# A feed-forward's output projection with held two-tile look-ahead, and modulation steps spread over its input products

## The chip, the cores and the metric

The kernel runs on one core of one Trainium2 chip. The metric is the device time of one execution in microseconds (us), as the median of several.

## What is computed

One layer of a diffusion backbone over 256 context and 512 latent tokens, 768 rows in all, with a model width of 1024. The part around the change is the first feed-forward, run on all 768 rows, and the modulation vectors of the later parts:

```python
mod = (sc @ w_mod[l] + b_mod[l]).reshape(-1, N_MOD, D_MODEL)      # 9 vectors of 1024, sc = silu(c)
modc = (scc @ w_mod[l] + b_mod[l]).reshape(1, N_MOD, D_MODEL)     # the same for the context rows
x = ada_out(x, swiglu(ada_in(x, mod, 0, norm_pre[l, 0]), ffn_w_in[l, 0], ffn_w_out[l, 0]),
            mod, 0, norm_post[l, 0], 0.5)
def swiglu(y, w_in, w_out):
    a, b = jnp.split(y @ w_in, 2, axis=-1)     # w_in 1024 x 5632
    return (jax.nn.silu(a) * b) @ w_out        # w_out 2816 x 1024
```

Behind it come the mLSTM and pooling mixer and a second feed-forward on the 512 latent rows. All of it is float32.

## The kernel before, in words

**Float32 products from parts.** Every operand of a large product is split into a high part (`split_hi`, a cast on ScalarE, line 81 in the profile's L81) and a low part (`split_lo`, a subtraction on VectorE, L78), and each product is three matmuls (`mm3`, L97 to L99; `mm3p`, L102, is the same with its order on TensorE held). So each weight tile costs one load of 512 KB, one cast and one subtraction before TensorE can use it.

**Input products (`Ffn.in_fast`, L359).** The hidden width of 2816 is 22 tiles `f` of 128. Tiles 3 to 21 go through `in_fast`: seven products of half size (a fast 2 x 2 matrix product) in place of eight, 84 matmuls of 384 columns. Sums of weight quarters come first (`first_sums`, `last_sums`), then their splits; a tile's split weights take 7 of the 8 buffers of tag `win`. The results are put together by VectorE additions (L379, L384, L388, L389, L392) and a multiplication (L393) and stored to DRAM as `g_f` (L490).

**Modulation steps (`mod_steps`, L666).** Seven blocks of 1024 modulation values (blocks 2 to 8) are computed on VectorE as a Python generator of 70 steps, ten to a block. Each of the first eight steps of a block loads 512 KB of `w_mod` into one of six `m4` buffers (L675) and issues one VectorE multiply-add (L677) for each stream: two streams (latent and context) for blocks 2 to 4, one for blocks 5 to 8. Step nine issues nothing; step ten issues eight matmuls with a vector of ones (L687), one scaling, and stores of the row. When block 4 is done, `begin_chain` prepares the parameters of the stage's end (eight transposes and eight small matmuls on TensorE, two loads of 256 KB and two row broadcasts). `filler(n)` takes n steps; it is called after each `in_fast` tile (two steps after tiles 4 to 11, three after tiles 12 to 21) and once after each output tile.

**Output projection (`out_pass`, L740).** Two passes, each over half of the rows (384) and over all 22 tiles, accumulate in six PSUM banks: 18 matmuls of 512 columns for each tile. `prepare(f)` loads and splits the weights `wos[f]` (load L748, unless they are kept from the first pass) and the hidden values `g_f` (load L751, into a buffer of tag `q3`). In the kernel before it stands right in front of the tile's products. The second pass begins with the four tiles whose weights are still in place. At the end of a pass, `done1` and `ada_tile` form the normalised rows of the next stage: squares (L148), scalings (L175, L179, L187), and for each row tile two "back" steps, each with four transposes on TensorE (L105), four activations on ScalarE (L199), a cast (L203) and a subtraction (L204). `Backs.tick` lets these steps run later, between the following tiles: one falls at the end of the first pass, five between the first tiles of the second.

**What sets the order.** The kernel is written for a tracing compiler that orders each engine's instructions itself: among those that its own estimate holds ready, the one traced first goes first. `keep_in_program_order` (in the code `pin`, `mm`, `tp`) holds an instruction behind the others so marked on its engine; `issue_after(ins)` keeps what a block issues on `ins`'s engine behind `ins`. Once built, each engine runs its list strictly in order, and so does the DMA queue of SP that issues nearly all loads and stores.

Of the kernel before, what the change touches and what calls it, by code (L numbers as in the profile page):

```python
# [8 lines left out]
F32 = mybir.dt.float32  # L9
# [34 lines left out]
def tile_layer(ctx: ExitStack, tc: tile.TileContext, x, c, ctxt, c_ctx, w_mod, b_mod, norm_pre, norm_post,  # L44
# [35 lines left out]
    def split_hi(src, hi):  # L80
        return S.copy(hi, src)  # L81

    def split_lo(src, hi, lo):
        return sub_to(V, lo, src, hi.bitcast(F32))
# [1 line left out]
    def part(pool=wpool, tag="win", n=D):  # L86
        return pool.tile([P, WIDE if tag == "win" else D], F32R, tag=tag, name=tag + "s")[:, 0:n]

    def split_w(src, pool=wpool, tag="win", to=None):

        hi, lo = to or (part(pool, tag), part(pool, tag))
        split_hi(src, hi)
        split_lo(src, hi, lo)
        return hi, lo

    def mm3(out_ap, wh, wl, xh, xl, first, last, **kw):
# [69 lines left out]
    x1_d = [dpool.tile([P, D], F32, name=f"x1_{t}") for t in range(4)]  # L166
    x2_d = [dpool.tile([P, D], F32, name=f"x2_{t}") for t in range(4)]

    def ada_tile(t, zs, z, halves, xr, gc, store, nxt, junk, half):


        r = rstd2(halves)
        parts = ([slice(0, D)] if zs is None else [slice(h * 512, (h + 1) * 512) for h in range(2)])
        for h, cs in enumerate(parts):
            mul = V.tensor_mul(z[:, cs], z[:, cs] if zs is None else zs[h], gc[:, cs])  # L175
            if nxt is None and t == NTT - 1:
                tc.keep_in_program_order(mul)
        for cs in parts:
            V.scalar_tensor_tensor(out=z[:, cs], in0=z[:, cs], scalar=r, in1=xr[:, cs], op0=ALU.mult, op1=ALU.add)  # L179
            if nxt is None:  # L180
                load(store[:, cs], z[:, cs])
        if nxt is None:
            return None
        if store is not None:
            load(store, z)
        r2 = rstd1(z, junk)
        V.tensor_scalar_mul(xr, z, r2)  # L187
        scale, shift = nxt
        ts = slice(t * P, (t + 1) * P)

        def back(q):
            yf = half()
            p = pt()
            for j in range(4):
                k = 4 * q + j
                tp(out=p[:, j * P:(j + 1) * P], in_=xr[:, k * P:(k + 1) * P], identity=ident)
            for j in range(4):
                k = 4 * q + j
                S.activation(out=yf[:, j * P:(j + 1) * P], in_=p[:, j * P:(j + 1) * P], func=AF.Identity,  # L199
                             scale=scale[:, k:k + 1], bias=shift[:, k:k + 1])  # L200
            ks = slice(4 * q, 4 * q + 4)
            ysrc = kc(yf)
            S.copy(yh[:, ks, ts], ysrc)  # L203
            V.tensor_sub(yl[:, ks, ts], ysrc, yh[:, ks, ts].bitcast(F32))  # L204

        return back

# [31 lines left out]
    class Ffn:  # L239
        def __init__(self, wi, wo_ap, tiles, c_lo, c_hi):  # L240
            self.wi, self.wo_ap, self.tiles, self.c_lo = wi, wo_ap, tiles, c_lo
            self.ncol = c_hi - c_lo
            self.g, self.w, self.wo, self.fast = {}, {}, {}, False

        def scope(self, pool, done, filler, junk):
            self.pool, self.done, self.filler, self.junk = pool, done, filler, junk
# [112 lines left out]
        def in_fast(self, f, between=lambda: None):  # L359

            n = self.n
            (xh, xl), (sh, sl), (uh, ul), x22p = self.w.pop(f, None) or self.last_sums(self.first_sums(f))
            lo, hi = slice(0, 512), slice(512, 1024)

            def product(q, wh, wl, y, first=True):
                wh, wl, (mh, ml) = kc(wh), kc(wl), self.moving[y]
                for k in range(4):
                    mm3(q[:, 0:n], wh[:, k], wl[:, k], mh[:, k], ml[:, k], first and k == 0, k == 3,
                        skip_group_check=not first)

            sg, cb, pu, pv = (self.two(x) for x in ("s", "cb", "pu", "pv"))
            p1, u2, p5, u3 = pu[:, 0:n], pu[:, n:2 * n], pv[:, 0:n], pv[:, n:2 * n]
            qa, qc, qb = pa(), pa(), pa()
            product(qa, xh[:, lo], xl[:, lo], "y11")
            S.copy(p1, qa[:, 0:n])
            product(qc, sh[:, lo], sl[:, lo], "t1")
            S.copy(p5, qc[:, 0:n])
            product(qb, sh[:, hi], sl[:, hi], "t2")
            V.tensor_add(u2, p1, qb[:, 0:n])  # L379
            between()  # L380
            product(qa, xh[:, hi], xl[:, hi], "y21", False)
            S.activation(out=sg[:, 0:n], in_=qa[:, 0:n], func=AF.Silu)
            product(qc, uh[:, hi], ul[:, hi], "y22", False)
            V.tensor_add(sg[:, n:2 * n], u2, qc[:, 0:n])  # L384
            S.activation(out=sg[:, n:2 * n], in_=sg[:, n:2 * n], func=AF.Silu)
            qd = pa()
            product(qd, uh[:, lo], ul[:, lo], "t3")
            V.tensor_add(u3, u2, qd[:, 0:n])  # L388
            V.tensor_add(cb[:, n:2 * n], u3, p5)  # L389
            qe = pa()  # L390
            product(qe, x22p[:, lo], x22p[:, hi], "t4")
            V.tensor_add(cb[:, 0:n], u3, qe[:, 0:n])  # L392
            V.tensor_mul(cb, cb, sg)  # L393
            self.finish(f, cb)
# [58 lines left out]
    with ExitStack() as sx:  # L453
        pool = sx.enter_context(tc.tile_pool(name="ffn1", bufs=6))

        def m4(dt=F32):
            return pool.tile([P, D], dt, tag="m4", name="m4")

        def q3(dt=F32):
            return pool.tile([P, NT], dt, tag="q3", name="q3", bufs=10)  # L460

        def sw(dt=F32):
            return pool.tile([P, D], dt, tag="sw", name="sw", bufs=2)
# [5 lines left out]
        def done1(t, qs, z, halves, xr):  # L469
            st = 1 if t < 2 else 0  # L470
            load(xr, ctxt[t * P:(t + 1) * P, :] if t < 2 else x[(t - 2) * P:(t - 1) * P, :])
            return ada_tile(t, qs, z, halves, xr, chain["g"][st], None if t < 2 else x1_d[t - 2], chain["y"][st], junk,
                            lambda: q3()[:, 0:512])

        blocks1 = ((0, 384), (384, 384))
        f1 = Ffn(ffn_w_in[0], ffn_w_out[0], range(NTT), 0, NT)
# [50 lines left out]
                    ws.append(r)  # L527
            return ws

        pin = tc.keep_in_program_order  # L530
        bgv = bg.rearrange("p (g k o) -> p g k o", g=3, o=1)

        class Split:
# [172 lines left out]
        steps = mod_steps()  # L706

        def filler(n):
            with tc.issue_after(sums_end.ins):
                for _ in range(n):  # L710
                    if next(steps, None) == 4:
                        begin_chain()

        def begin_chain():
            mix_params()
            query_key()
            chain["g"] = [bc_row(m4(), (2, st)) for st in range(2)]
            cols = columns("ycol1", [(4, 0), (3, 0), (4, 1), (3, 1)])
            chain["y"] = [(cols[0], cols[1]), (cols[2], cols[3])]
# [10 lines left out]
        with tc.issue_after(last_y.ins):  # L730
            f1.w[3] = f1.last_sums(f1.first_sums(3, raws3))
        sums_end = rest()
        for f in range(3, NF):
            f1.in_fast(f)
            filler(3 if f >= 12 else 2 if f > 3 else 0)


        wos = {}
# [1 line left out]
        def out_pass(half, order, tail, homes, z, xr, before, backs):  # L740
            c0 = 384 * half
            qs = [(pa(), pa()), (pa(), pa()), (pz(), pz())]
            gs = {}

            def prepare(f):
                if f not in wos:
                    r = raw()
                    load(r, f1.wo_ap[f * P:(f + 1) * P, :])  # L748
                    wos[f] = split_w(r, to=homes[f]() if f in homes else None)
                r = q3()[:, 0:384]  # L750
                load(r, g_d[f][:, c0:c0 + 384])  # L751
                g = q3(F32R)
                gs[f] = split_w(r, to=(g[:, 0:384], g[:, 384:NT]))

            def product(f, i, h, mm3):
                (gh, gl), (wh, wl) = gs[f], wos[f]
                ts, cs = slice(i * P, (i + 1) * P), slice(512 * h, 512 * h + 512)
                mm3(qs[i][h], gh[:, ts], gl[:, ts], wh[:, cs], wl[:, cs], f == order[0], f == order[-1])

            for f in order[:-tail]:  # L760
                prepare(f)
                for i in range(3):
                    for h in range(2):
                        product(f, i, h, mm3)
                before.tick()
                filler(1)
            for f in order[-tail:]:
                prepare(f)
            for i in range(3):
                t, halves = 3 * half + i, small(2)  # L770
                for h in range(2):
                    for f in order[-tail:]:
                        product(f, i, h, mm3p)
                    square_to(halves[:, h:h + 1], qs[i][h], junk[:, 512 * h:512 * h + 512])
                    backs.tick()
                backs.add(done1(t, qs[i], z[:, i], halves, xr(i)))

        def rows3(tag):
            return pool.tile([P, 3, D], F32, tag=tag, name=tag + "z", bufs=1)
# [1 line left out]
        backs, first_backs = Backs(4), Backs(4)  # L781
        xr1 = rows3("tl")
        order = list(range(NF))
        out_pass(0, order, 2, {}, rows3("th"), lambda i: xr1[:, i], Backs(0), first_backs)
        for f in order[:-4]:
            wos.pop(f)
        order = order[-4:] + order[-5::-1]
# [606 lines left out]
```

## Time and profile before

| | us |
|---|---|
| median of 3 runs | 1189.13 |
| lowest, highest | 1185.16, 1192.81 |
| the profiled execution, own time | 1192.41 |
| its span, first to last instruction | 1190.7 |
| mean granted TensorE clock over the span | 0.978 of full speed |

Times in the rows below are counted from the start of the span of the profiled execution. A wait is put down to the instruction that ended it (behind the arrow `<-`). The granted clock is a share of full speed; 1.00 is 2.4 GHz, 0.50 is 1.2 GHz. A few per cent of the matmul records may be missing, so counts of matmuls are a little low.

### The profile page before, as it was taken

To read this page: it belongs to the slowest core of one execution; us is meant where nothing else is said; L and a number is where in the kernel's file an instruction comes from. 1 tells how busy PE (TensorE), PEld (TensorE's weight loads), DVE (VectorE), ACT (ScalarE), POOL (GpSimd) and SP (SyncE) were. 2 spreads that over 40 slices of the span, in tenths; PEclk is the share of its full clock that TensorE was granted. 3 is DMA by queue.
4 is the path that set the end of the run, shared out by engine and by line. 5 is a ranking of instruction groups with operands and counts; after the bars stand their busy time and mean duration, and the time that the engine had idled before them with its cause. 6 is when DMAs were issued, how large, how long until landed. Compare 5 with 4: busy or idle time off the path is not lost.

```text
span 1190.7 us, 17232 instructions
## 1 busy us (share of the span) xinstructions
PE 1123.2 (94%) x6610; PEld 1012.6 (85%) x6610; DVE 895.5 (75%) x1315; ACT 530.3 (45%) x910; POOL 104.6 (9%) x139
## 2 busy tenths in 40 slices
PE   4999999997999999779999799999999999999996
PEld 3899999996999787557889688887989999999995
DVE  3799988989798756424553877785899998888865
ACT  4544333341434333434455466556664444444431
POOL 4000000000000000100020505421000000000001
PEclk9999999998999999889999899999999999999999
DMA  9934436354576887335642211224334433333321
GB/s 300 297 103 133 132 107 217 103 169 141 155 226 227 294 290 254 123 101 178 210 126 58 58 45 63 80 89 142 126 101 121 132 107 107 107 107 107 98 80 72
DMA packets 152672, 169.25 MB, mean 142 GB/s; under 512 B 7414, under 2 KB 125686, under 8 KB 152588
## 3 DMA queue, kind: packets, MB, share of 16 engines
q1 hardware_dynamic: 152540, 168.12, 44.5%
q8 instruction: 52, 0.85, 0.3%
q14 instruction: 32, 0.26, 0.1%
q10 hardware_dynamic: 48, 0.01, 0.0%
HBM read 153.12 MB, written 14.98 MB: 141 GB/s over the span
## 4 chain that ended last, share of the span: by engine, by line
PE 78%; DVE 8%; issue 4%; ACT 4%; POOL 3%; DMA 1%; DVEq 0%; ACTq 0%; POOLq 0%; SPq 0%
PE pa L98 16%; PE pa L97 16%; PE pa L99 16%; PE pa L102 8%; PE pz L102 5%; PE pz L97 4%; PE pz L98 4%; PE pz L99 4%; PE pt L102 2%; DVE m L677 2%; DVE wins L78 1%; PE pt L105 1%; ACT wins L81 1%; POOL sm L143 1%; ACT q L199 1%
## 5 line engine op out<-in xcount | busy, mean ns | idle before, releaser
L98 PE MATMUL pa<-yh,wins 128*128 128x256 f32 (+1 forms) x768 | 238.4, 311 | 2.7 <-DVE wins L78 2.7
L78 DVE TENSOR_TENSOR wins<-raw,wins 128x1024 fp32r<-128x1024 f32 (+1 forms) x145 | 158.0, 1090 | 107.9 <-ACT wins L81 75.7
L97 PE MATMUL pa<-yh,wins 128*128 128x256 f32 (+1 forms) x768 | 238.1, 310 | 0.7 <-ACT yh L81 0.4
L99 PE MATMUL pa<-yl,wins 128*128 128x256 f32 (+1 forms) x768 | 238.1, 310 | 0.0
L81 ACT CAST wins<-raw 128x1024 fp32r<-128x1024 f32 (+1 forms) x147 | 136.7, 936 | 130.8 <-PE pz L98 69.9
L98 PEld LDWEIGHTS pa<-yh,wins 128*128 128x128 f32 x768 | 146.5, 191 | 5.1 <-DVE wins L78 4.6
L97 PEld LDWEIGHTS pa<-yh,wins 128*128 128x128 f32 x768 | 146.2, 190 | 4.3 <-issue 2.1
L99 PEld LDWEIGHTS pa<-yl,wins 128*128 128x128 f32 x768 | 146.6, 191 | 0.5
L97 PE MATMUL pa<-th,wins 128*128 128x384 f32 (+1 forms) x388 | 121.8, 315 | 0.7 <-ACT wins L81 0.7
L99 PE MATMUL pa<-tl,wins 128*128 128x384 f32 (+1 forms) x388 | 122.4, 316 | 0.0
L98 PE MATMUL pa<-th,wins 128*128 128x384 f32 (+1 forms) x388 | 122.1, 315 | 0.0
L81 ACT CAST wins<-sw 128x1024 fp32r<-128x1024 f32 x78 | 81.7, 1048 | 54.1 <-DVE sw L78 34.1
L78 DVE TENSOR_TENSOR wins<-sw,wins 128x1024 fp32r<-128x1024 f32 x78 | 95.4, 1223 | 10.3 <-PE pa L98 7.0
L677 DVE SCALAR_TENSOR_TENSOR m<-m,sc,m 128x1024 f32<-128x1024 f32 x80 | 101.2, 1281 | 2.5 <-DMA m<-in_w_mod_dram 2.3
L102 PE MATMUL pa<-yh,wins 128*128 128x512 f32 (+2 forms) x352 | 96.8, 362 | 0.0
L97 PE MATMUL pa<-wins,q 128*128 128x512 f32 x152 | 60.0, 412 | 19.6 <-ACT q L81 19.6
L97 PEld LDWEIGHTS pa<-th,wins 128*128 128x128 f32 x388 | 73.1, 189 | 1.2 <-ACT wins L81 1.1
L99 PEld LDWEIGHTS pa<-tl,wins 128*128 128x128 f32 x388 | 73.3, 189 | 0.1
L98 PEld LDWEIGHTS pa<-th,wins 128*128 128x128 f32 x388 | 73.3, 189 | 0.0
L102 PEld LDWEIGHTS pa<-yh,wins 128*128 128x128 f32 x352 | 61.8, 190 | 9.1 <-issue 2.2
L98 PE MATMUL pa<-wins,q 128*128 128x512 f32 x152 | 63.8, 420 | 1.0 <-DVE q L78 1.0
L99 PE MATMUL pa<-wins,q 128*128 128x512 f32 x152 | 63.1, 415 | 0.0
(376 smaller groups left out, 2176.8 us busy)
## 6 DMA issues: line engine op xcount, KB each, us to landing
raw<-in_ffn_w_in_dram SPq DMA_DIRECT2D x87, 512.0 KB
raw<-in_ffn_w_out_dram SPq DMA_DIRECT2D x62, 512.0 KB
m<-in_w_mod_dram SPq DMA_DIRECT2D x57, 512.0 KB
g<-q SPq DMA_DIRECT2D x22, 384.0 KB
q<-g SPq DMA_DIRECT2D x44, 192.0 KB
raw<-in_w_in_dram SPq DMA_DIRECT2D x16, 512.0 KB
raw<-in_w_mod_dram SPq DMA_DIRECT2D x11, 512.0 KB
raw<-in_w_out_dram SPq DMA_DIRECT2D x16, 256.0 KB
```

What stands on the lines that cost most here:

```text
L78: return eng.tensor_tensor(out=out_ap, in0=a, in1=b, op=ALU.subtract)
L81: return S.copy(hi, src)
L97: T.matmul(out_ap, lhsT=wh, rhs=xh, start=first, stop=False, **kw)
L98: T.matmul(out_ap, lhsT=wl, rhs=xh, start=False, stop=False, **kw)
L99: T.matmul(out_ap, lhsT=wh, rhs=xl, start=False, stop=last, **kw)
L102: return tc.keep_in_program_order(T.matmul(*args, **kw))
L105: return tc.keep_in_program_order(T.transpose(**kw))
L143: G.tensor_tensor(out=r, in0=ms, in1=mhalf[:, 0:n], op=ALU.pow)
L199: S.activation(out=yf[:, j * P:(j + 1) * P], in_=p[:, j * P:(j + 1) * P], func=AF.Identity, scale=scale[:, k:k + 1], bias=shift[:, k:k + 1])
L677: V.scalar_tensor_tensor(out=accs[st], in0=w, scalar=sc[:, st * KD + k:st * KD + k + 1], in1=accs[st], op0=ALU.mult, op1=ALU.add)
```

## The change

`split_w` and `ada_tile` get a `keep` argument, by which the splits of `out_pass` and the activations, casts and subtractions of the back steps are held in program order on ScalarE and VectorE. In `out_pass`, the first two tiles are prepared ahead of the loop, and inside it tile `f + 2` is prepared before the products of tile `f`. In the first pass, tile 0's weights go to the two `sw` buffers, which held weight sums before, in place of `win` buffers.

The modulation steps of the input products no longer come in groups after a tile. `in_fast` calls `self.tick` after two of its VectorE additions (L379 and L389); three of every four calls take a single step, whose VectorE instructions are kept behind that addition. That makes 27 steps in tiles 4 to 21 instead of 46. The first pass of the output projection takes two steps after every third tile and one after the others (27 instead of 20), and the second pass the remaining 16 instead of 4. The old order of all steps behind `sums_end` is dropped.

```diff
-    def split_w(src, pool=wpool, tag="win", to=None):
+    def split_w(src, pool=wpool, tag="win", to=None, keep=lambda ins: ins):
         hi, lo = to or (part(pool, tag), part(pool, tag))
-        split_hi(src, hi)
-        split_lo(src, hi, lo)
+        keep(split_hi(src, hi))
+        keep(split_lo(src, hi, lo))
...
     def ada_tile(..., half, keep=lambda ins: ins):      # done1 passes pin
-                S.activation(out=yf[...], in_=p[...], func=AF.Identity, ...)
+                keep(S.activation(out=yf[...], in_=p[...], func=AF.Identity, ...))
-            S.copy(yh[:, ks, ts], ysrc)
-            V.tensor_sub(yl[:, ks, ts], ysrc, yh[:, ks, ts].bitcast(F32))
+            keep(S.copy(yh[:, ks, ts], ysrc))
+            keep(V.tensor_sub(yl[:, ks, ts], ysrc, yh[:, ks, ts].bitcast(F32)))
...
     in_fast:
-            V.tensor_add(u2, p1, qb[:, 0:n])
+            self.tick(V.tensor_add(u2, p1, qb[:, 0:n]))
...
-            V.tensor_add(cb[:, n:2 * n], u3, p5)
+            self.tick(V.tensor_add(cb[:, n:2 * n], u3, p5))
...
         def filler(n):
-            with tc.issue_after(sums_end.ins):
-                for _ in range(n):
-                    if next(steps, None) == 4:
-                        begin_chain()
+            for _ in range(n):
+                if next(steps, None) == 4:
+                    begin_chain()
...
-        for f in range(3, NF):
+        f1.in_fast(3)
+        count = iter(range(100))
+
+        def mod_tick(ins):
+            if next(count) % 4 < 3:
+                with tc.issue_after(ins.ins):
+                    filler(1)
+
+        f1.tick = mod_tick
+        for f in range(4, NF):
             f1.in_fast(f)
-            filler(3 if f >= 12 else 2 if f > 3 else 0)
...
-                    wos[f] = split_w(r, to=homes[f]() if f in homes else None)
+                    wos[f] = split_w(r, to=homes[f]() if f in homes else None, keep=pin)
...
-                gs[f] = split_w(r, to=(g[:, 0:384], g[:, 384:NT]))
+                gs[f] = split_w(r, to=(g[:, 0:384], g[:, 384:NT]), keep=pin)
...
-            for f in order[:-tail]:
+            for f in order[:2]:
                 prepare(f)
+            for f, later in zip(order[:-tail], order[2:]):
+                prepare(later)
                 for i in range(3):
                     for h in range(2):
                         product(f, i, h, mm3)
                 before.tick()
-                filler(1)
-            for f in order[-tail:]:
+                filler(2 if half == 0 and f % 3 == 0 else 1)
+            for f in order[len(order) - tail + 2:]:
                 prepare(f)
...
-        out_pass(0, order, 2, {}, rows3("th"), lambda i: xr1[:, i], Backs(0), first_backs)
+        out_pass(0, order, 2, {0: lambda: (sw(F32R), sw(F32R))}, rows3("th"), lambda i: xr1[:, i], Backs(0), first_backs)
```

## Rows read from the trace of the kernel before

**Rows 1.** Windows by stage: PE, PEld, DVE, ACT, POOL busy us (count), clock, DMA, GB/s.

```profile
278.00:304.00 26.00, 18.60 (x68) 16.24 (x68) 22.51 (x26) 6.65 (x10) 0.00 (x0) 0.74 0.30 99
392.30:486.70 94.40, 92.55 (x408) 74.35 (x404) 58.14 (x65) 33.11 (x51) 2.61 (x5) 1.00 0.79 271
486.70:544.00 57.30, 37.68 (x136) 28.00 (x137) 21.16 (x30) 23.98 (x52) 3.92 (x8) 0.82 0.33 110
```

**Rows 2.** Waits of PE, 250 to 396 us: total, times, longest, in us.

```profile
PE pt L687 <- issue: 4.0, 1, 4.0
PE pa L98 <- DVE wins L78: 2.7, 2, 2.3
PE pa L97 <- ACT q L81: 1.8, 1, 1.8
PE pa L97 <- ACT wins L81: 0.7, 1, 0.7
```

**Rows 3.** Timeline of DVE and PE: start, duration, instruction, count, idle before.

```profile
275.46 4.87 DVE L677 SCALAR_TENSOR_TENSOR m<-m,sc,m 128x1024 f32<-128x1024 f32 x4
...
281.52 0.69 PE L98 MATMUL pa<-yh,wins 128*128 128x384 f32 x1 [2.26 <-DVE wins L78]
```

**Rows 4.** Windows of line L677 alone: length, DVE busy (count), clock, DMA, GB/s.

```profile
265.00:294.50 29.50, 18.85 (x16) 0.88 0.41 136
107.10:392.30 285.20, 78.14 (x62) 0.98 0.52 167
392.30:486.70 94.40, 20.50 (x16) 1.00 0.79 271
```

**Rows 5.** ACT timeline, first copy (L375) of two neighbouring input tiles.

```profile
121.80 0.48 ACT L375 COPY q<-pa 128x384 f32<-128x384 f32 x1 [1.02 <-PE pa L99]
...
136.54 0.48 ACT L375 COPY q<-pa 128x384 f32<-128x384 f32 x1 [1.01 <-PE pa L99]
```

**Rows 6.** Window of two tile periods without modulation steps; columns as rows 1.

```profile
159.20:188.68 29.48, 29.48 (x171) 28.39 (x170) 21.04 (x30) 11.07 (x17) 0.00 (x0) 1.00 0.48 157
```

**Rows 7.** Windows at half and at full clock; columns as rows 1.

```profile
280.73:287.56 6.83, 6.04 (x19) 6.04 (x20) 4.75 (x6) 1.46 (x2) 0.00 (x0) 0.50 0.38 119
294.39:301.21 6.82, 6.36 (x16) 4.66 (x17) 6.75 (x8) 1.59 (x3) 0.00 (x0) 0.50 0.24 78
306.00:312.83 6.83, 6.83 (x41) 6.83 (x40) 5.32 (x8) 2.87 (x5) 0.00 (x0) 1.00 0.26 78
502.60:509.43 6.83, 5.94 (x14) 4.69 (x15) 1.16 (x2) 0.83 (x2) 0.00 (x0) 0.50 0.34 106
523.08:526.49 3.41, 3.41 (x10) 2.65 (x9) 0.00 (x0) 0.00 (x0) 0.00 (x0) 0.50 0.77 270
548.00:554.83 6.83, 6.83 (x31) 5.54 (x30) 2.41 (x4) 2.95 (x4) 0.00 (x0) 1.00 0.71 233
```

**Rows 8.** Waits of PE, 476 to 545 us: total, times, longest, in us.

```profile
PE pa L97 <- ACT q L81: 17.8, 6, 3.7
```

**Rows 9.** Timeline of SP and ACT around one stall of the second pass.

```profile
502.68 0.38 SPq L751 DMA_DIRECT2D q<-g  x1
...
510.43 1.04 ACT L81 CAST wins<-raw 128x1024 fp32r<-128x1024 f32 x1 [6.99 <-PE pz L98]
511.38 1.50 ACT L199 ACTIVATE q<-pt,ycol 128x128 f32<-128x128 f32 x4
512.91 0.62 ACT L203 CAST yh<-q 128x512 fp32r<-128x512 f32 x1
513.43 0.51 ACT L81 CAST q<-q 128x384 fp32r<-128x384 f32 x1
```

**Rows 10.** DMA view of the first pass, 392.3 to 486.7 us.

```profile
DMA packets 9391, 25.56 MB, mean 271 GB/s; under 512 B 1151, under 2 KB 4262, under 8 KB 9385
```

**Rows 11.** The busiest window of the first pass; columns as rows 1.

```profile
410.00:420.00 10.00, 10.00 (x45) 8.11 (x44) 7.84 (x9) 3.79 (x5) 0.00 (x0) 1.00 1.00 376
```

**Rows 12.** Waits of the SP queue, 107.1 to 392.3 us: total, times, longest.

```profile
SPq L675 <- DVE m L677: 51.9, 21, 7.2
```

More of the change, by code (lines that the diff above doesn't have):

```diff
@@ L167, in tile_layer, with ada_tile @@
     x2_d = [dpool.tile([P, D], F32, name=f"x2_{t}") for t in range(4)]
-    def ada_tile(t, zs, z, halves, xr, gc, store, nxt, junk, half):
+    def ada_tile(t, zs, z, halves, xr, gc, store, nxt, junk, half, keep=lambda ins: ins):
         r = rstd2(halves)
@@ L198, in back @@
                 k = 4 * q + j
-                S.activation(out=yf[:, j * P:(j + 1) * P], in_=p[:, j * P:(j + 1) * P], func=AF.Identity,
-                             scale=scale[:, k:k + 1], bias=shift[:, k:k + 1])
+                keep(S.activation(out=yf[:, j * P:(j + 1) * P], in_=p[:, j * P:(j + 1) * P], func=AF.Identity,
+                                  scale=scale[:, k:k + 1], bias=shift[:, k:k + 1]))
             ks = slice(4 * q, 4 * q + 4)
             ysrc = kc(yf)
-            S.copy(yh[:, ks, ts], ysrc)
-            V.tensor_sub(yl[:, ks, ts], ysrc, yh[:, ks, ts].bitcast(F32))
+            keep(S.copy(yh[:, ks, ts], ysrc))
+            keep(V.tensor_sub(yl[:, ks, ts], ysrc, yh[:, ks, ts].bitcast(F32)))
         return back
@@ L242, in __init__ @@
             self.ncol = c_hi - c_lo
-            self.g, self.w, self.wo, self.fast = {}, {}, {}, False
+            self.g, self.w, self.wo, self.fast, self.tick = {}, {}, {}, False, lambda ins: None
         def scope(self, pool, done, filler, junk):
@@ L457, in m4 @@
             return pool.tile([P, D], dt, tag="m4", name="m4")
+        pin = tc.keep_in_program_order
         def q3(dt=F32):
@@ L472, in done1 @@
             return ada_tile(t, qs, z, halves, xr, chain["g"][st], None if t < 2 else x1_d[t - 2], chain["y"][st], junk,
-                            lambda: q3()[:, 0:512])
+                            lambda: q3()[:, 0:512], pin)
         blocks1 = ((0, 384), (384, 384))
@@ L528, in mod_loads @@
             return ws
-        pin = tc.keep_in_program_order
         bgv = bg.rearrange("p (g k o) -> p g k o", g=3, o=1)
```

## The prediction

> **What bounds the kernel now.** I read the profile's page first: TensorE (PE) is busy in nearly every slice, but its row dips twice in the part that the change touches, and the granted clock dips with it. The windows by stage then price the dips [rows 1]: in 278 to 304 us PE is busy for 18.60 of 26.00 us at a mean clock of 0.74 while VectorE (DVE) is busy for 22.51; in 486.7 to 544 us, where the second output pass begins, PE is busy for 37.68 of 57.30. Between them, in the first output pass, PE is busy for 92.55 of 94.40. So PE bounds this part, and it loses time at three places; the waits of PE, the timelines and the waits by name tell why.
>
> *Input products.* PE waits four times [rows 2]: 4.0 for the matmuls that end a modulation block (L687), 2.7 in two waits for weight splits on DVE, 0.7 for a cast; the 1.8 belongs to the output projection. The timeline shows the cause of the longest split wait [rows 3]: four modulation multiply-adds in a row, 4.87 us, stand on DVE before the split, and PE is idle for 2.26. The steps come in clumps, 16 multiply-adds in 29.5 us [rows 4]. One tile takes 14.74 us of PE (the same copy at 121.80 and 136.54, [rows 5]). Without modulation DVE works 21.04 us in two such periods, 10.52 a tile [rows 6]. A multiply-add takes 78.14 / 62 = 1.26 us [rows 4]. Two two-stream steps a tile make 10.52 + 4 x 1.26 = 15.6 us, three make 18.1: both over 14.74.
>
> *Clock.* After the idle 2.26 us the granted clock is 0.50, which is 1.2 of 2.4 GHz, from 280.73 for 6.83 us, and again from 294.39 behind the 4.0 wait [rows 7].
>
> *Second pass.* PE waits six times, 17.8 us in total, for the same thing, a cast of `g` on ScalarE (ACT) [rows 8]. One stall is enough to see why [rows 9]: SP issued that load at 502.68, the tile began with the cast at 513.43, and what stood ahead of it on ACT was the back step's four activations (1.50) and its cast (0.62), which wait for PE's transposes. The data had 10 us to land; ACT's order was late.
>
> **The change part by part.** The sum is made in the profiled execution's own time, 1192.41 us (span 1190.7 and 1.71 around it), which is 3.28 above the median of 1189.13 and within the runs' spread.
>
> (a) *Single steps.* Three of four additions let a step in, so 1.5 a tile: DVE has 10.52 + 3 x 1.26 = 14.30 us in a period of 14.74 while all steps issue, and as two steps in ten issue no multiply-add, 13.5 on average. No more than two multiply-adds (2.5 us) stand together, and the L687 matmuls come two calls behind the last of them. That removes 4.0 + 2.7 + 0.7 = 7.4 us of waits, and the two stretches of half clock: half of the 6.04 + 6.36 us that PE works in them, 6.2 (19 matmuls in 6.04 us against 41 in 6.83 at full clock, [rows 7], is about half the rate). A multiply-add now waits behind its addition, and so for PE; behind it on DVE stand the next tile's splits, which tile f + 1 wants only when its products begin, and on SP the loads that want its buffer (rival E). What is late next is DVE itself, with 0.4 us a tile to spare. I charge 1.5; the ends are 0 (in [rows 6] DVE keeps up) and 7.4 (the waits stay). Less than nothing is left out, as the waits are counted whole.
>
> (b) *Start of the first pass.* Tile 0 in the `sw` buffers needn't wait for a `win` buffer and is prepared, with tile 1, before the loop: the 1.8 wait for its cast goes [rows 2]. Its cover is tile 21's products; without it, 1.8 stays.
>
> (c) *Held look-ahead in the second pass.* `g` and weights of tile f + 2 are cast ahead of the back step that follows tile f. PE needs 18 matmuls a tile; 31 in 6.83 us [rows 7] make that 4.0 us, so each cast has 4 us or more in hand against the 2.1 us of activations and cast in front of it. Five of the six waits fall between tiles and go: 17.8 - 3.7 (the longest, the first) = 14.1. The first stays, since the back step at the end of the first pass is traced ahead of tile 18's split and is now held there. What holds a cast also holds what is queued behind it: on ACT the squares and back steps, for which only PE's transposes two tiles later wait. Three half-clock stretches behind these waits go too: 502.60, 523.08, and one of 3.41 more like the latter. 14 + 10 + 10 matmuls in 5.94 + 3.41 + 3.41 = 12.76 us would take 34 / 4.54 = 7.5 at 31 in 6.83: 5.3 us. The first wait and its half clock I leave at no gain; at best they give 3.7 + 3.4 (half of 6.83, as the like stretches in [rows 7]), at worst another 1.5 (activations, [rows 9]) comes ahead of the cast.
>
> (d) *Moved work.* By trace order the 27 steps in the input products are blocks 2 and 3 and seven of block 4, so 62 multiply-adds there [rows 4] become 16 + 16 + 14 = 46, 16 in the first pass become 22, and the second takes the last 12. On DVE the first pass has 58.14 busy [rows 1] + 6 x 1.26 = 66 of 92.6 us: room. `begin_chain` (TensorE transposes, two loads, two broadcasts) and one L687 group move with their cost from one PE-bound stage to the next: sum nothing. SP gets five more loads of 0.52 MB in the first pass, and the chain's four of 1.6 MB together: 25.56 [rows 10] + 2.6 + 1.6 = 29.8 MB. At the stage's mean of 271 GB/s that is 110 us, 15.6 over its 94.40; at the 376 GB/s of its busiest window [rows 11] it is 79, hidden. Since that window is what the engines give at share 1.00, I take the near end, and charge 2 us for loads that come late, and 1 for L687 matmuls that wait in PE's order for multiply-adds whose loads are late. A gain is excluded: apart from (b), PE has no idle time there.
>
> The Trainium skill (DMA: Bandwidth & Descriptors, Bandwidth) puts the ceiling of the 16 engines at 435 GB/s; by it (d) would take 69 us, and the charge of 2 would be nothing. The measured 376 at a share of 1.00 lies below it, so the measurement decides and the charge stays.
>
> Sum: 7.4 + 6.2 + 1.8 + 14.1 + 5.3 = 34.8 us gained; 1.5 + 2 + 1 = 4.5 charged; net 30.3. That is 1162.1 from the profiled execution and 1158.8 from the median. I forecast 1160.
>
> **The rivals.**
>
> *A: only the output projection gains.* The in-order DVE list comes out with new clumps, since 14.30 of 14.74 leaves little room. For it: waits of up to 2.3 us for splits already. Against: two multiply-adds together are half of today's four. Without (a), the gain is 1.8 + 14.1 + 5.3 - 3 = 18.2: 1171.
>
> *B: the first pass becomes bound by loads.* For it: 271 GB/s on average, at a share of 0.79 [rows 1]. Against: 376 in its busiest window. 34.8 - 1.5 - 15.6 = 17.7: 1171.
>
> *C: the five equal stalls are a shortage of buffers.* A weight cast that waits for a `win` buffer until a tile's products end would hold all behind it, and an order that casts earlier would wait at the same place. For it: the weight cast in [rows 9] did wait 6.99 us for PE. Against: it ended 3 us before PE went on, and PE went on behind the `g` cast. The 14.1 + 5.3 would stay: 1189.1 - 30.3 + 19.4 = 1178. The Trainium skill (Perfetto Trace Analysis, Optimization Strategy) reads a gap that repeats as a possible lack of room for the next tile; by that rule it is this case. The trace agrees only for the weights.
>
> *D: the built order hardly changes.* The compiler had already placed splits early where its estimate let it: about 1189.
>
> *E: slower.* In the input products, SP's queue is strictly in order and a `w_mod` load stands in it until a multiply-add frees a buffer: 51.9 us in 21 waits already, the longest 7.2 [rows 12]. Now steps can't run ahead of their addition, so a load can wait a whole call, 14.74 / 2 = 7.4 us, and the weight loads behind it too. Against: five raw buffers at two a tile let weights lead by up to two tiles. If such a wait reaches PE, it costs 7.4; from the fifth on (37 against 30.3) the change loses. Six make 1189.1 - 30.3 + 44.4 = 1203.
>
> **How the numbers follow.** Forecast 0.60 (its own range 1150 to 1170), A 0.12, B 0.09, C 0.05, D 0.04, E 0.10. The range goes from 1149 (no charge falls due and most of the first wait of the second pass with its half clock goes as well: 1158.8 - 4.5 - 7.1 = 1147 at best) to 1182; it takes in A, B and C and leaves out D, E and a few hundredths below. About 1% is what a measurement tells here, so faster means below 1177.2: forecast, A, B make 0.81; D, C and a little of the rest make 0.09 for the same; E is 0.10.
>
> **What would show it.** After: PE waits in the input products sum to under 2 us, no half clock there, multiply-adds stand in twos; the five waits for `g` casts of some 2.9 us are gone, and only the one at the seam of the passes stays, with half clock behind it; the first pass keeps its PE row full at a DMA share over 0.85. Wrong would be: gaps before L687 or `wins` in the first pass (B), stalls at the same five places (C), new waits for `raw` loads in the input products (E).

## The result and the profile after

| | before | after |
|---|---|---|
| median, us | 1190.66 | 1173.02 |
| lowest, highest of 4 runs | 1185.16, 1192.81 | 1170.85, 1175.41 |
| the profiled execution, own time | 1192.41 | 1170.85 |

The ratio is 0.986 (95% interval 0.982 to 0.990), so the change gains 17.6 us in the medians and 21.6 between the profiled executions. The forecast was 1160 and its net gain 30.3: the direction was right, and the medians moved by a little over half of that. A second set of runs gave 1173.35, 0.985 (0.983 to 0.987). Line numbers of after lie one higher at the modulation steps (L678 answers to L677, L676 to L675, L688 to L687, L704 to L703) and eight in the output projection (L756 to L748, L759 to L751).

I read the pages first, the rows of PE and of its clock in 40 slices of the span: before, then after.

```profile
PE   4999999997999999779999799999999999999996
...
PEclk9999999998999999889999899999999999999999
```

```profile
PE   4999999999999999599899799999999999999996
...
PEclk9999999999999999799999899999999999999999
```

One deep dip is left, in slice 17 (468 to 497 us), and a shallow one in slice 20; the 7 in slice 23 lies behind the change and is in the page of before as well. The windows by stage say what each part gained or lost (columns: length, then PE, PEld, DVE, ACT, POOL busy with counts, clock, DMA share, GB/s).

```profile
278.00:304.00 26.00, 26.00 (x151) 24.91 (x151) 18.73 (x27) 9.43 (x15) 0.00 (x0) 1.00 0.30 92
107.10:373.50 266.40, 266.40 (x1525) 263.14 (x1523) 227.01 (x291) 99.64 (x143) 3.82 (x4) 1.00 0.43 138
373.50:476.10 102.60, 97.69 (x430) 77.03 (x431) 69.70 (x77) 35.58 (x55) 6.38 (x8) 0.98 0.82 298
478.51:492.16 13.65, 5.32 (x12) 3.73 (x13) 8.94 (x12) 7.01 (x16) 3.87 (x7) 0.50 0.50 160
```

The 26 us in which PE worked 18.60 at a clock of 0.74 [rows 1] are now full at 1.00, and so are all 266.40 us of the input products from tile 4 on: no wait of PE is left in them. The first pass is less full than it was: PE works 97.69 of 102.60 us, where it was 92.55 of 94.40. And the seam between the passes has a stretch of 13.65 us at half clock. As a ledger between the two profiled executions:

| part | before | after | difference |
|---|---|---|---|
| start to the first product of the first pass | 394.2 | 373.5 | -20.7 |
| first pass, to the first transpose behind it | 93.3 | 102.6 | +9.3 |
| from there to the first product of the second pass | 4.3 | 9.5 | +5.2 |
| from there to the end | 698.9 | 683.5 | -15.4 |
| sum | 1190.7 | 1169.1 | -21.6 |

The steps now stand as forecast, in twos behind an addition, L379 or L389 (DVE timeline; the lines left out are splits and other additions):

```profile
320.94 0.55 DVE L379 TENSOR_TENSOR q<-q,pa 128x384 f32<-128x384 f32 x1
321.40 2.48 DVE L678 SCALAR_TENSOR_TENSOR m<-m,sc,m 128x1024 f32<-128x1024 f32 x2
...
328.28 0.55 DVE L389 TENSOR_TENSOR q<-q 128x384 f32<-128x384 f32 x1
328.75 2.48 DVE L678 SCALAR_TENSOR_TENSOR m<-m,sc,m 128x1024 f32<-128x1024 f32 x2
```

The waits of PE from 476.3 to 600 us answer to [rows 8]: the five stalls of some 2.9 us are gone, the first has grown from 3.7 to 8.9, and one wait for a cast has come that was not there, 2.8 us at the end of the second pass.

```profile
PE pa L97 <- ACT q L81: 8.9, 1, 8.9
PE pa L102 <- ACT q L81: 2.8, 1, 2.8
PE pt L105 <- DVE tlz L187: 1.9, 1, 1.9
PE pa L98 <- DVE q L78: 1.2, 1, 1.2
```

**The seam.** ACT's timeline shows what the cast of tile 18's `g` (L81 at 485.10) now stands behind:

```profile
478.60 1.06 ACT L148 ACTIVATE junk<-thz 128x1024 bf16<-128x1024 f32 x1 [4.12 <-DVE thz L179]
...
479.83 0.60 ACT L148 ACTIVATE junk<-pz 128x512 bf16<-128x512 f32 x1
...
480.42 0.59 ACT L148 ACTIVATE junk<-pz 128x512 bf16<-128x512 f32 x1
...
480.99 1.51 ACT L199 ACTIVATE q<-pt,ycol 128x128 f32<-128x128 f32 x4
482.53 0.62 ACT L203 CAST yh<-q 128x512 fp32r<-128x512 f32 x1
484.04 1.06 ACT L148 ACTIVATE junk<-thz 128x1024 bf16<-128x1024 f32 x1 [0.90 <-DVE thz L179]
...
485.10 0.50 ACT L81 CAST q<-q 128x384 fp32r<-128x384 f32 x1
```

Before, the same stretch of ACT's list was shorter: the cast came one activation behind the back step.

```profile
488.14 1.50 ACT L199 ACTIVATE q<-pt,ycol 128x128 f32<-128x128 f32 x4 [1.26 <-PE pt L105]
489.68 0.62 ACT L203 CAST yh<-q 128x512 fp32r<-128x512 f32 x1
490.20 1.05 ACT L148 ACTIVATE junk<-thz 128x1024 bf16<-128x1024 f32 x1
...
491.25 0.49 ACT L81 CAST q<-q 128x384 fp32r<-128x384 f32 x1
491.65 0.59 ACT L148 ACTIVATE junk<-pz 128x512 bf16<-128x512 f32 x1
```

In after, the two squares of the third row tile's products (`pz`) and the square of its normalised row (`thz`, 484.04), which waits for VectorE, have come ahead of the cast. The four transposes of the back step (476.12) are all that PE has to do meanwhile. The load isn't what is late: SP issued it at 474.49 (and the next one only at 484.48, behind the store of a row tile, L185, that waited 7.5 us for VectorE), and the cast follows the instruction before it on ACT with no wait of its own.

**The end of the first pass.** SP's waits and its timeline from 430 to 462 us:

```profile
SPq L704 <- ACT m L692: 11.4, 1, 11.4
```

```profile
438.27 0.80 SPq L756 DMA_DIRECT2D raw<-in_ffn_w_out_dram  x2
451.35 1.12 SPq L704 DMA_DIRECT2D row<-m  x4
...
455.15 0.51 SPq L756 DMA_DIRECT2D raw<-in_ffn_w_out_dram  x1
```

The store of a finished modulation row (L704, 1 to 2 KB) waits 11.4 us for the scaling on ACT (L692) that makes the row, and in that time SP issues nothing. So the last tile's weights are asked for only at 455.15, their cast is late, and PE waits 1.69 and 0.81 us in the tail of the pass (the products of its last tiles), with 3.41 us at half clock (464.86). At the end of the second pass a store waits 5.9 us for VectorE in the same way; PE waits 2.83 and 0.82 us, with half clock again at 574.08. There the last `g` cast stands on ACT behind casts of the next stage's weights, whose loads came late too. The two windows at half clock (columns as above):

```profile
464.86:468.27 3.41, 3.10 (x7) 2.48 (x8) 2.15 (x3) 0.69 (x2) 0.00 (x0) 0.50 1.03 411
...
574.08:577.50 3.42, 3.15 (x7) 2.49 (x8) 2.13 (x3) 1.04 (x3) 0.00 (x0) 0.50 1.02 271
```

The DMA view of the first pass (40 slices) shows the hole: two slices at nothing or next to it behind one at 50, between 445 and 453 us.

```profile
DMA  9847789998999999207999999999100699999947
GB/s 325 256 137 249 292 303 358 407 341 271 380 396 392 355 382 287 109 0 224 337 351 379 404 409 384 403 401 406 50 0 2 184 348 355 394 418 406 386 198 232
DMA packets 11437, 30.55 MB, mean 298 GB/s; under 512 B 1257, under 2 KB 5137, under 8 KB 11428
```

### The profile page after: what moved, and what is told of

Its sections match the earlier page's. It is cut to its first block, busy times and chain, and to the rows that moved or that the text cites. A ratio compares the mean times of both kernels' runs of the same rounds, so it can differ in the third digit from the quotient of the medians.

```text
span 1169.1 us, 17262 instructions
## 1 busy us (share of the span) xinstructions
PE 1111.0 (95%) x6610; PEld 1004.8 (86%) x6610; DVE 894.8 (77%) x1315; ACT 530.6 (45%) x910; POOL 106.4 (9%) x139
## 4 chain that ended last, share of the span: by engine, by line
PE 47%; DVE 6%; ACT 2%; DMA 1%; issue 1%; POOL 1%; SPq 0%; DVEq 0%; ACTq 0%; POOLq 0%
PE pa L102 9%; PE pa L98 7%; PE pa L99 7%; PE pa L97 7%; PE pz L102 4%; PE pz L97 3%; PE pz L98 3%; PE pz L99 3%; PE pt L102 3%; PE pt L105 1%; DVE wins L78 1%; DMA raw<-in_w_in_dram 1%; ACT junk L148 1%; DMA q<-g 0%; DVE z L179 0%
## 5 line engine op out<-in xcount | busy, mean ns | idle before, releaser
L78 DVE TENSOR_TENSOR wins<-raw,wins 128x1024 fp32r<-128x1024 f32 (+1 forms) x144 | 156.6, 1087 | 70.5 <-PE pa L98 39.8
L81 ACT CAST wins<-raw 128x1024 fp32r<-128x1024 f32 (+1 forms) x146 | 136.2, 935 | 110.5 <-PE pa L99 36.9
L678 DVE SCALAR_TENSOR_TENSOR m<-m,sc,m 128x1024 f32<-128x1024 f32 x80 | 100.2, 1278 | 9.6 <-DMA m<-in_w_mod_dram 5.9
L81 ACT CAST wins<-sw 128x1024 fp32r<-128x1024 f32 x78 | 81.7, 1047 | 48.9 <-PE pa L99 35.5
L78 DVE TENSOR_TENSOR wins<-sw,wins 128x1024 fp32r<-128x1024 f32 x78 | 95.2, 1221 | 10.7 <-PE pa L98 7.0
L97 PE MATMUL pa<-wins,q 128*128 128x512 f32 x148 | 55.3, 407 | 8.9 <-ACT q L81 8.9
L102 PE MATMUL pa<-yl,wins 128*128 128x512 f32 (+2 forms) x176 | 62.4, 355 | 0.5 <-DVE yl L78 0.5
L98 PE MATMUL pa<-wins,q 128*128 128x512 f32 x148 | 59.3, 400 | 1.2 <-DVE q L78 1.2
```

Source lines behind the costliest of these rows:

```text
L78: return eng.tensor_tensor(out=out_ap, in0=a, in1=b, op=ALU.subtract)
L97: T.matmul(out_ap, lhsT=wh, rhs=xh, start=first, stop=False, **kw)
L98: T.matmul(out_ap, lhsT=wl, rhs=xh, start=False, stop=False, **kw)
L102: return tc.keep_in_program_order(T.matmul(*args, **kw))
L678: V.scalar_tensor_tensor(out=accs[st], in0=w, scalar=sc[:, st * KD + k:st * KD + k + 1], in1=accs[st], op0=ALU.mult, op1=ALU.add)
```

## The experiments

Each kernel computes the whole result. Ratios are to the kernel before, run on the same chip, with 95% intervals. My theory was: single steps gain in the input products, the look-ahead in the second pass, and two things take gain back: the seam, and SP's order at the ends of the passes.

**The steps alone.** `out_pass` as before; the step calls, and the numbers of steps in the passes, as after.

```diff
+            self.tick(V.tensor_add(u2, p1, qb[:, 0:n]))
...
-            filler(3 if f >= 12 else 2 if f > 3 else 0)
...
-                filler(1)
+                filler(2 if half == 0 and f % 3 == 0 else 1)
```

> The changed step calls alone, output projection as in the kernel before. My theory (the step calls gave about 15 us in the input products, more than forecast; the passes gave the five stalls back but lost at their ends): about 1176 us, ratio 0.988, with the five waits of about 2.9 us for g casts in the second pass, a first wait at the seam of about 3.7 us and no wait in the input products. Rival (the first pass is bound by loads, now that seven more steps load there): waits of several us in the first pass, 1183 us or more.

Measured: 1209.57, ratio 1.016 (1.013 to 1.018): slower than before by 19 us. My 1176 was wrong, and the time and the waits are those of the rival. PE has no wait from 100 to 374 us, as in after, but many in the first pass, 374 to 498 us:

```profile
PE pa L98 <- DVE q L78: 7.7, 3, 3.1
PE pa L97 <- ACT q L81: 6.6, 3, 3.7
PE pa L102 <- ACT q L81: 2.2, 2, 1.8
```

```profile
374.40:497.50 123.10, 106.11 (x430) 81.73 (x429) 69.68 (x76) 34.44 (x54) 4.52 (x7) 0.92 0.76 260
```

The window of the pass (columns as above) speaks against the rival's cause as far as bytes go: the DMA engines' share is 0.76 on average at 260 GB/s, no more than the 0.79 at 271 of the kernel before [rows 1]. So the single steps do what they were priced for, and what they move into the passes costs more than they gain, where tiles are prepared right in front of their products.

**The output projection alone.** The held look-ahead and the `sw` buffers for tile 0, the old step groups (edits as in the diff of the change).

> The held two-tile look-ahead alone, modulation steps as in the kernel before. My theory (the five stalls go, 19 us with their half clock and 1.8 at the start, but the seam of the passes grows by 6 to 7 us and its half clock by 3, from the held order itself): about 1180 us, ratio 0.991, one wait of 8 to 9 us at the seam, and the 7.4 us of waits in the input products as before. Rival (the seam grows because modulation steps now run into it): a seam wait of 3.7 us, about 1170 us.

Measured: 1176.68, 0.988 (0.985 to 0.991). The waits in the input products are those of [rows 2] again, the products at the ends of the passes wait for nothing, and the seam has its long wait:

```profile
PE pa L97 <- ACT q L81: 10.0, 3, 9.0
PE pt L688 <- issue: 4.0, 1, 4.0
PE pa L98 <- DVE wins L78: 2.7, 2, 2.3
```

So the longer seam belongs to the new `out_pass`, the tail waits to the moved steps. The steps add only 1176.68 - 1173.02 = 3.7 us to this half of the change, and as the intervals of the two ratios overlap, even that is hardly clear of the noise.

**Back steps not held.**

```diff
-                            lambda: q3()[:, 0:512], pin)
+                            lambda: q3()[:, 0:512])
```

> The changed kernel with the back steps' activations, casts and subtractions no longer held; the splits stay held. Theory one (the g cast of the second pass's first tile is late because it is traced behind the row tiles' ends of the first pass, so it stands behind the square of the third row tile on ACT): the seam wait stays at 8 us or more, time within 3 us of the changed kernel. Rival (holding the back steps is what delays it): the seam wait falls to about 3.7 us, 8 us less than the changed kernel, about 1165.

Measured: 1172.88, 0.984 (0.982 to 0.987), as after; the seam's wait is 9.3. The hold of the back steps isn't what makes it.

**Row stores on another queue.** GpSimd issues the stores of L704, so that nothing of SP's stands behind them.

```diff
-                    load(rows[(blk, st)][:, cs], res[g:g + 1])
+                    nc.gpsimd.dma_start(rows[(blk, st)][:, cs], res[g:g + 1])
```

> The changed kernel with the stores of the modulation rows issued by GpSimd in place of SP. Theory one (at the end of each pass SP's queue stands behind a row store that waits for its block's end, 11.4 us in the first pass and 5.9 in the second, so the last tiles' weights and g land late and PE waits 2.5 and 3.65 us with 3.4 us of half clock behind each): both waits go, 6 to 9 us less than the changed kernel, about 1165. Rival (the loads are late because the DMA engines are full): the waits stay within 1 us, time as the changed kernel.

Measured: 1164.93, 0.978 (0.976 to 0.980), 8.4 under the run of after on the same chip (1173.35). The windows (columns as above) from 440 to 451 us, after first, then this kernel:

```profile
440.00:451.00 11.00, 11.00 (x54) 8.42 (x53) 6.86 (x8) 2.97 (x5) 0.96 (x1) 1.00 0.53 207
```

```profile
440.00:451.00 11.00, 11.00 (x50) 8.96 (x49) 9.34 (x11) 4.64 (x7) 0.96 (x1) 1.00 1.03 402
```

The hole in the transfers is filled, and the waits of PE for `q` casts at both tails are gone; the 8.9 at the seam stays. One wait is new: 2.5 us for the chain's load of `w_k` at the start of the first pass.

**The seam prepared ahead.** Tiles 18 and 19 are prepared for the second pass before the first pass's last products.

```diff
-            gs = {}
+            gs = ahead.setdefault(half, {})
...
+            if half == 0:
+                for f in order[-4:-2]:
+                    prepare(f, 1, ahead.setdefault(1, {}))
             for i in range(3):
```

> The changed kernel with the first two tiles of the second pass prepared ahead of the first pass's last products, so their g casts stand ahead of the row tiles' ends on ACT. Theory one (the seam's 8.90 us wait and its 13.65 us of half clock come from that cast's place): the wait at the start of the second pass goes, the 1.9 us wait for the transposes stays, 9 to 14 us less than the changed kernel, about 1161. Rival (the casts only move and the next cast, of the third tile, holds PE as long): less than 4 us less.

Measured: 1163.10, 0.977 (0.975 to 0.979), 10.25 under after. The 8.9 is gone, and the tail waits stay, a little longer (400 to 600 us):

```profile
PE pa L102 <- ACT q L81: 6.0, 2, 3.8
PE pz L97 <- DVE thz L175: 1.4, 1, 1.4
```

**Both.** The two edits above together.

> Both edits, the second pass's first tiles ahead of the first pass's end and the row stores on GpSimd. If the two losses are separate and are all that was missing, the gains add up: 15 to 20 us less than the changed kernel, about 1155. If one of the theories above falls, no better than the other edit alone.

Measured: 1153.02, 0.969 (0.967 to 0.970), 20.3 under after, where 8.4 and 10.25 alone add up to 18.7: two separate losses. This is the fastest kernel of the study, with 37 us under before. Its window over all that the change touches:

```profile
60.00:620.00 560.00, 553.89 (x3029) 509.47 (x3028) 429.92 (x542) 238.59 (x381) 42.51 (x74) 1.00 0.55 179
```

PE is idle for 6.1 of 560 us, at a clock of 1.00.

**A step at every call.** 36 steps in the input products instead of 27, and one a tile in the first pass.

```diff
-            if next(count) % 4 < 3:
-                with tc.issue_after(ins.ins):
-                    filler(1)
+            with tc.issue_after(ins.ins):
+                filler(1)
...
-                filler(2 if half == 0 and f % 3 == 0 else 1)
+                filler(1)
```

> Every one of the two calls of an input tile takes a step (36 in place of 27), and each tile of the first pass one. Theory one (it was the clumps that cost the kernel before its waits, not the sum of DVE's work): 10.52 + 4 x 1.26 = 15.6 us of DVE against 14.74 of PE while two-stream blocks run, but for eight steps in ten only (14.6 on average), so waits in the input products stay under 2 us, and the time is that of the changed kernel within 4 us. Rival (DVE's sum decides): DVE falls behind by 0.9 us a tile while steps issue, and PE waits for splits in the input products, 5 us or more with half clock behind them.

Measured: 1162.39, 0.977 (0.974 to 0.980): 10.6 under after's median, more than I had expected. The input products hold the extra steps with no wait of PE, and the tail waits are gone, since fewer loads and row stores are left to the passes; the seam's 9.0 stays, and 2.7 come at the start of the first pass.

**All three.**

> The first tiles of the second pass early, the row stores on GpSimd, and every call of an input tile taking a step, so nine fewer steps in the passes. Theory one (the three losses are separate: seam, row stores, steps in the passes): less than the 1153 of the first two edits together, by the loads that the passes lose: 1145 to 1150. Rival (the gain of taking every call was that row stores fell elsewhere, so it is the same loss as that of the row stores): 1153 within 3 us.

Measured: 1153.72, 0.969 (0.967 to 0.972): no better than the two edits without it. So moving the row stores to another queue and leaving fewer steps to the passes mend the same loss, and between these two places of the steps there is nothing to choose once SP isn't blocked.

**Still more steps.** All three edits, and every fourth call takes two steps (45 in the input products).

```diff
-                filler(1)
+                filler(2 if next(count) % 4 == 3 else 1)
```

> All three edits, and every fourth call of an input tile taking two steps: 45 in place of 36, about as many as in the kernel before (46), but spread. Theory one (clumps cost, the sum hardly does): DVE has 10.52 + 62 x 1.26 / 18 = 14.86 us a tile against 14.74, so 2 us at most in the whole stage, and the time is that of the run without the doubled calls within 3 us. Rival (past the point where DVE's sum exceeds PE's, waits and half clock return at once): waits of 5 us or more in the input products, 5 to 12 us slower.

Measured: 1155.14, 0.971 (0.969 to 0.973). From 107.1 to 378.6 us VectorE is busy for 241.17 of 271.50, and PE waits under 1 us in all:

```profile
107.10:378.60 271.50, 270.57 (x1552) 265.08 (x1551) 241.17 (x305) 100.63 (x146) 13.69 (x22) 1.00 0.55 169
```

Nearly as many steps as before stand here (45 against 46), and the 7.4 us of waits don't come back. It was their clumps that cost, not their sum.

**The steps alone, `w_mod` loads on GpSimd's queue.**

```diff
-                    load(w, w_mod[k * P:(k + 1) * P, blk * D:(blk + 1) * D])
+                    nc.gpsimd.dma_start(w, w_mod[k * P:(k + 1) * P, blk * D:(blk + 1) * D])
```

> The step calls alone, as in the run that came out at 1209.6, with the loads of w_mod issued by GpSimd in place of SP. Theory one (without look-ahead each tile's g load stands in SP's queue behind w_mod loads that wait for a buffer, and PE waits): the waits in the first pass, 16.5 us there, fall below 6, and the time comes to 1190 or less. Rival (the DMA engines are too full for the load to land in time, whichever queue issues it): the waits stay, 1203 or more.

Measured: 1199.50, 1.008 (1.005 to 1.010), between the readings. PE's waits in the first pass fall from 16.5 to 7.9 us (374 to 480 us), but the first transposes of the seam now wait 8.4 (374 to 540 us):

```profile
PE pa L97 <- ACT q L81: 23.3, 7, 4.8
PE pt L105 <- DVE tlz L187: 8.4, 1, 8.4
```

The timelines of POOL (first) and DVE have the reason. The addition that opens the row tile's closing work (L175, 485.71) stands on VectorE behind a multiply-add (484.50) that waits for its load, and GpSimd issued that load only at 480.61, when it had waited 5.40 us for an earlier multiply-add. From the addition the chain goes on over ACT's square and GpSimd's small operations to the scaling (L187) and the transposes.

```profile
480.61 0.53 POOL L675 DMA_DIRECT2D m<-in_w_mod_dram  x1 [5.40 <-DVE m L677]
```

```profile
484.50 1.28 DVE L677 SCALAR_TENSOR_TENSOR m<-m,sc,m 128x1024 f32<-128x1024 f32 x1 [1.50 <-DMA m<-in_w_mod_dram]
485.71 1.28 DVE L175 TENSOR_TENSOR thz<-pa,m 128x512 f32<-128x512 f32 x2
...
491.59 0.75 DVE L187 TENSOR_SCALAR tlz<-thz,sm 128x1024 f32<-128x1024 f32 x1 [0.76 <-POOL sm L143]
```

So part of the loss of the steps alone is SP's order; how the rest divides stays open.

**No hold at all.** The fastest kernel without `pin` on splits and back steps (all `keep=pin` of the change dropped).

> The best kernel so far (first tiles of the second pass early, row stores on GpSimd, 1153.0) with nothing held any more: the splits and back steps are only traced two tiles ahead. Theory one (being traced ahead is what removed the five waits; the hold adds little): no g cast wait above 1 us in the second pass, 1153 within 4 us. Rival (without the hold weight casts that wait for a buffer come ahead of the back steps' casts on ACT, and the waits return): waits of 1 us or more at three or more tiles of the second pass, 1160 or more.

Measured: 1154.90, 0.969 (0.968 to 0.970), the same as with it. No `g` cast holds PE in the second pass, so there the place in the trace, two tiles ahead, does the work. The hold isn't without effect: at the start of the first pass a wait has come back (100 to 600 us) that the kernel with the hold doesn't have.

```profile
PE pa L97 <- ACT q L81: 3.7, 1, 3.7
```

## Why the prediction was right and wrong

Forecast and measured differences, part by part in the ledger's rows, are these:

| part | forecast | measured |
|---|---|---|
| input products: -7.4 - 6.2 - 1.8 + 1.5, and 3.6 of moved PE work | -17.5 | -20.7 |
| first pass: 3.0 of that work, charges of (d) +3 | +6.0 | +9.3 |
| seam | 0 | +5.2 |
| second pass and rest: -14.1 - 5.3, and 0.6 of that work | -18.8 | -15.4 |
| sum | -30.3 | -21.6 |

The 3.6 are `begin_chain`'s sixteen matmuls (2.4 in the trace of before) and two groups of L687 (0.6 each), which leave the input products. The first pass gets the chain and one group, the second pass the other group; I had named one group only. I had counted this work as nothing in the sum, as it is. The multiply-adds came out as 48 in the input products, 22 in the first pass and 10 behind it, where I had 46, 22 and 12.

**(a) Single steps: right.** The waits and both stretches of half clock are gone, and the charge of 1.5 wasn't due; of the 3.2 us that the stage gave beyond the table, the other 1.7 stay open. VectorE is busy for 227.01 of 266.40 us, 12.6 in a period of 14.74, where I had 13.5. Rival A falls by the windows of after, and rival E's place too: no PE wait there, and SP's waits for `w_mod` buffers in the input products are 30.4 us in 12, down from 51.9 in 21 [rows 12], as fewer loads are issued there; a single wait is no shorter on average.

**(b) Start of the first pass: right.** The 1.8 is gone; 0.56 for a subtraction of VectorE (L78) has come in its place.

**(c) Held look-ahead: right for the five stalls, wrong for the first.** The step that failed is "The first wait and its half clock I leave at no gain", with 1.5 more as the worst. It became 8.9, and the half clock around it 13.65 us, of which 7.1 lie inside the wait. I had counted on ACT the four activations and the cast of the back step, which stand ahead of the `g` cast on both sides. I left out the squares of the last row tile. I had said that what is held holds what is queued behind it; here it was the cast that landed behind others. The experiment with the seam prepared ahead prices the whole wait, the 3.7 of before with it, at 10.25 us. What puts the cast behind the squares stays open. The hold of the back steps is excluded. The place in the trace alone can't be it, since the kernel before traces tile 18's preparation at the same place, as the first of the second pass, and has the cast ahead of these squares. The hold of the splits was not tried alone.

Rival C falls: the five gaps went with the same buffers. (The weight cast of [rows 9], which spoke against it, ended 2.5 us before PE went on at 513.99, not 3.) The Trainium skill (Perfetto Trace Analysis, Optimization Strategy) names a lack of room as a possible reason of a repeating gap. In this case's traces it isn't the reason: the gaps of up to 2.9 us went with no buffer added to the second pass, since the casts were late by their place on ACT.

**(d) Moved work: the bytes right, the charge too small, and for the wrong reason.** The transfers of the pass were forecast at 29.8 MB and are 30.55 over a window 8.2 us longer, and the engines had room: slices run at up to 418 GB/s, so the 376 of [rows 11] was no ceiling, and others stand at nothing. Rival B, a bound by bytes, falls. The sign that I had named is not there, though: the share is 0.82 and not over 0.85, and PE's row isn't full. What I charged as "2 us for loads that come late" is 1.69 + 0.81 us of waits in the first pass's tail and some 1.5 of half clock (half of the 3.10 us that PE works in it). The second pass's tail, for which I had charged nothing, has 2.83 + 0.82 us of waits and some 1.6 of half clock (half of 3.15). Taking the stores out of SP's list gave 8.4 back. The 1 us for L687 matmuls wasn't due, as no wait of PE in the pass is at one.

The Trainium skill (DMA: Bandwidth & Descriptors, Issuing engines are not separate DMA queues) has it that issuing from several engines saves only the issuing time. Here the four stores' issue took 1.12 us and the wait in front of it 11.4, so the runs show more to gain where an issue waits. The Trainium skill (Perfetto Trace Analysis, DMA Optimizations) says that it may make sense to give loads one issuing engine and stores another. The run bears this out for the row stores, the only ones that were moved.

I had seen that a moved step takes its loads onto SP, and not that its stores go with them, which wait for the end of the block on ACT or VectorE. Rival E named the mechanism, SP's order, with another instruction and another place.

The two costs, 8.4 and 10.25, are more than the 12.7 us by which the medians miss the forecast's net gain: part of each was in the sum as a charge, or in the kernel before as the 3.7 at the seam. Without them the kernel takes 1153.02, 4 us above the 1149 to which the range went.

The range held the result by luck in part. 1173.02 lies above the 1150 to 1170 that I gave the forecast itself, and nearer to the 1171 of A and B than to my 1160; that part of the range was there for A, B and C, none of which happened.

## What to carry to other kernels

When a step moves, list every instruction that it puts on an in-order queue with what that instruction waits for: a store of 1 KB that waits 11 us for its producer stops every load behind it, though the DMA engines are idle. When a loop gets look-ahead, look at the seam to the stage before it as a case of its own: here the first tile's cast queued behind the last stage's closing work until its preparation was traced ahead of that. And judge the parts together: here one half alone lost 19 us, the other alone gained 13.5, and the two gained 17.6.

## What the runs showed that I had not expected

- The granted clock fell to 0.50 (1.2 GHz) at 464.86 for 3.41 us behind waits of only 1.69 and 0.81 us, and at 574.08 for 3.42 behind 2.83 and 0.82; around the 8.9 us wait it was low for 13.65, in which PE worked 5.32. This stretch begins at 478.51, inside the wait, which ends at 485.64. In the kernel before, too, the low stretch that I put after the idle 2.26 us begins at 280.73 [rows 7], before PE goes on at 281.52 [rows 3].
- Multiply-adds that wait for their `w_mod` load hold what stands behind them on VectorE: with these loads on GpSimd's queue, a row tile's addition came so late that the transposes downstream waited 8.4 us.
- The DMA engines' share doesn't tell their rate. With the row stores on GpSimd they carried 402 GB/s over 11 us at a share of 1.03, and after itself 411 over 3.41 us (464.86); but over the 3.42 us from 574.08 it was 271 at 1.02, and the window that I had taken as their measure has 376 at 1.00.
